# One copy and one subtraction for both heads' q or k, stacked by transfers, and attention's loads on GpSimd's queue

## The chip, the cores and the metric

The kernel runs on one core of one Trainium2 chip. The engines are TensorE (PE, with weight loads shown apart as PEld), VectorE (DVE), ScalarE (ACT), GpSimd (POOL) and SyncE (SP), which here only issues transfers. The metric is device microseconds of one execution; lower is better. A verdict is taken from several executions of both kernels on the same chip.

## The reference

A trunk of two layers on 512 positions of width 1024, batch 1, everything in float32. Each layer projects a modulated norm of x once and splits the columns among three head groups: A (4 heads, differential attention, rotary), B (6 heads, rotary, a mixture of three dilated windows) and C (6 heads, with a learned forgetting bias). Then come an output projection and a gated MLP with a causal convolution.

```
sc = jax.nn.silu(c)
for layer in range(DEPTH):
    mod = sc @ w_mod[layer] + b_mod[layer]             # 6 x 1024: shifts, scales, gates
    h = rmsnorm(x, g_attn[layer]) * (1.0 + scale1) + shift1
    proj = h @ w_in                                    # qa ka va qb kb vb qc kc vc fz
    qa, ka = apply_rope(...); qb, kb = apply_rope(...) # A and B turn q and k; C does not
    oa = diff_attention(qa, ka, va, lam)
    ob = dilated_mixture_attention(qb, kb, vb)
    oc = forgetting_attention(qc, kc, vc, cumsum(log_sigmoid(fz + forget_bias)))
    x = x + gate1 * (concat(oa, ob, oc) @ w_out)
    h = rmsnorm(x, g_mlp[layer]) * (1.0 + scale2) + shift2
    up = h @ w_up                                      # u and g, 2816 wide each
    x = x + gate2 * ((silu(conv3(g)) * u) @ w_down)
return rmsnorm(x, g_final)
```

## The kernel before

**Precision by parts.** A product of float32 values is made of three fast products: each operand is split into a high part, a copy rounded to the type that TensorE reads fast (`fp32r`), and a low part, the value less its high part. `mm3` issues high by high, low by high and high by low. A split is one copy on ACT (`split_gen`, L240; for weights L174) and one subtraction on DVE (L242; for weights L186).

**Data flow.** Activations stand as 128 features by 512 positions. Weights come from DRAM in loads of 512 KB or a little less. `Weights.dma` (L148) issues them in the fixed order of `plan` into three buffers (`raww`); `hi` and `lo` split them into `whi` and `wlo`. `pump` keeps the loads two ahead of their use. The modulation of layers 0 and 1 is computed on DVE from loads named `rawm` (L214, L217), 24 of them during layer 0's attention, the rest during the MLPs; the start of the program does the first 16 with loads named `mu`, partly with products on POOL (L1036).

**Attention.** `ORDER` pairs the sixteen heads: B0 B1 A0 C0 A1 C1 B2 C2, two heads to a pair (for A two, with two maps each). While a pair's blocks of scores, softmax and products with V run, TensorE is filled up with the projections of the next pair's q and k (`qkps`, three buffers in PSUM shared with V's projections `vps`) and of V. `qk_post` takes a projection out of PSUM and makes from it the tiles `qk` that the scores multiply. For A and B it first turns them: a copy `qf` (L456), a pair of transfers that swaps rows into `sw` (L458, L459), and three DVE operations (L462, L464, L466). Transfers are started by SP's queue, in the order of the program.

**The stacked tiles.** A score needs three products. For B and C the kernel puts two of them into one matmul by stacking 64 rows of one part over 64 rows of another. For head h of a pair, with rows R[h] of the projection:
- q of B: `res[h]` has the high part in rows R[h] and the low part in the other 64 rows.
- k of B: `res[h]` has the high part twice, `res[2+h]` the low part twice.
- C is alike, but `res[2+h]` has only one half of 64 rows, and four rows of the forgetting bias below it that come by a transfer (L443).

`stack_gen` makes these tiles with operations on 64 rows: the high part on ACT (L423), the low part on DVE (L420), and the second copies on ACT (L434, L436). B is read from `qf` in SBUF, C straight from the projection in PSUM.

**What sets the order.** Nothing is ordered by hand. The code is written as generators that are advanced in turn; a scheduler then places each engine's instructions by priority and by its own estimate of when each can start, and adds the semaphores that they need. Each transfer ends on one of eight semaphores of its kind (named DMAHW for SP's and ACT's queues, DMASW for GpSimd's), taken in turn.

In the change, `dma` (L148) and `mod_stream` (L214) name the queue of the loads, `stack_gen` is rewritten, and `layer_attn` sets the queue around its loop over blocks.

Of the kernel before, what the change touches and what calls it, by code (L numbers as in the profile page):

```python
# [8 lines left out]
F32 = mybir.dt.float32  # L9
F32R = mybir.dt.float32r  # L10
AF = mybir.ActivationFunctionType
ALU = mybir.AluOpType
# [11 lines left out]
ORDER = [(k, "AABBBCCC".index(k) + int(n)) for k, n in "B0 B1 A0 C0 A1 C1 B2 C2".split()]  # L24
# [6 lines left out]
def kernel(  # L31
# [25 lines left out]
    nc = tc.nc  # L57
    PS = bass.MemoryType.PSUM
    V, A, T, G = nc.vector, nc.scalar, nc.tensor, nc.gpsimd
# [15 lines left out]
    def tmp(name, tag):  # L75
        if tag == "rp":
            return rpp[0].tile([128, SEQ], F32, tag=tag, name=name, bufs=4)
        return tp.tile([128, SEQ], F32, tag=tag, name=name, bufs=4)
# [37 lines left out]
    for l in range(DEPTH):  # L116
# [16 lines left out]
        for m in range(KC):  # L133
            for b in range(0, FC, 8):
                n = min(8, FC - b)
                plan += [(wdown[l, m, :, 128 * b:128 * (b + n)], 128 * n, "wp" if m < 7 else "hs")]

    class Weights:
        def __init__(self):
            self.raw, self.w = {}, {}  # L140
            self.nd = self.nh = self.nl = self.nu = 0
            self.pt = None

        def dma(self, upto):
            while self.nd < min(upto, len(plan)):
                src, n, at = plan[self.nd]
                t = rawp.tile([128, 4 * VZ], F32, tag="raw", name="raww")
                nc.sync.dma_start(out=t[:, 0:n], in_=src)  # L148
                self.raw[self.nd] = t
                self.nd += 1  # L150

# [57 lines left out]
    W = Weights()  # L209

    def mod_stream(l, ci):
        part, m = divmod(ci, 8)
        raw = mrp.tile([128, 1024], F32, tag="raw", name="rawm")
        nc.sync.dma_start(out=raw, in_=wmod[l, ci])  # L214
        yield
        dst = modc[:, l, ci:ci + 1]
        V.tensor_tensor_reduce(out=raw, in0=raw, in1=scb, scale=1.0, scalar=bm[:, l, ci:ci + 1],  # L217
                               op0=ALU.mult, op1=ALU.add, accum_out=dst)
        yield
        yield  # L220
        yield
        if m < 7:
            return
        c = slice(8 * part, 8 * part + 8)
        if part in (1, 4):
            g = gA if part == 1 else gM
            V.scalar_tensor_tensor(out=scl[:, l, part // 4, :], in0=modc[:, l, c], scalar=1.0,
                                   in1=g[:, l, :], op0=ALU.add, op1=ALU.mult)
# [10 lines left out]
    def split_gen(src, hi, lo):  # L239
        A.activation(out=hi, in_=src, func=AF.Copy)  # L240
        yield
        V.tensor_tensor(out=lo, in0=src, in1=hi.bitcast(F32), op=ALU.subtract)  # L242
        yield
# [23 lines left out]
    H0, H1 = slice(0, 64), slice(64, 128)  # L267
# [98 lines left out]
    def layer_attn(l, ap, mods, st, rt0):  # L366
        h = st.h
# [45 lines left out]
                vvs[q] = ap.tile([128, 4, 4, 128], F32R, tag="vv", name="vv", bufs=2)  # L413
                aux.append(v_post(q, lambda tb: pss[tb // nb][:, 256 * (tb % nb):256 * (tb % nb) + 256]))

        def stack_gen(src, side, res, pair=None):
            R = (H0, H1)

            def sub(out, h):
                V.tensor_tensor(out=out, in0=src[R[h]], in1=res[h][R[h]].bitcast(F32), op=ALU.subtract)  # L420

            for h in range(2):
                A.activation(out=res[h][R[h]], in_=src[R[h]], func=AF.Copy)  # L423
                yield
                if side == 0:
                    sub(res[h][R[1 - h]], h)
                elif pair is None:
                    sub(res[2 + h][R[h]], h)
                else:
                    sub(res[2 + h][H0], h)  # L430
                yield
                dup = res[h][R[1 - h]] if side == 1 else res[2 + h][H0] if pair is not None else None
                if dup is not None:
                    A.activation(out=dup, in_=src[R[h]], func=AF.Copy)  # L434
                if side == 1 and pair is None:
                    A.activation(out=res[2 + h][R[1 - h]], in_=res[2 + h][R[h]].bitcast(F32), func=AF.Copy)  # L436
                yield
            if pair is not None:
                while not aug:
                    yield  # L440
                for h in range(2):
                    c = 24 * side + 4 * (2 * (pair - 5) + h)
                    nc.sync.dma_start(out=res[2 + h][64:68, :].bitcast(F32), in_=aug[0][c:c + 4, :].bitcast(F32))  # L443
                yield

        def qk_post(idx, side, ps, kind):
            n = 2 + 2 * side if kind == "B" else 4
            res = [ap.tile([128, SEQ], F32R, tag="qk", name="qk", bufs=QKB) for _ in range(n)]
            qks[idx, side] = res
            if kind == "C":  # L450
                yield from stack_gen(ps, side, res, ORDER[idx][1])
                qkdone.add((idx, side))
                return
            tb = rope_tile(kind)
            qf = tmp("qf", "rp")
            A.activation(out=qf, in_=ps, func=AF.Copy)  # L456
            sw = tmp("sw", "rp")
            nc.sync.dma_start(out=sw[0::2, :], in_=qf[1::2, :])  # L458
            nc.sync.dma_start(out=sw[1::2, :], in_=qf[0::2, :])  # L459
            for _ in range(5):  # L460
                yield
            V.tensor_tensor(out=qf, in0=qf, in1=tb[:, 0, :], op=ALU.mult)  # L462
            yield
            V.tensor_tensor(out=sw, in0=sw, in1=tb[:, 1, :], op=ALU.mult)  # L464
            yield
            V.tensor_tensor(out=qf, in0=qf, in1=sw, op=ALU.add)  # L466
            yield
            if kind != "A":
                yield from stack_gen(qf, side, res)
            else:  # L470
                hi, lo = sw.bitcast(F32R), qf.bitcast(F32R)
                yield from split_gen(qf, hi, lo)
                yield
                for m in range(4):
                    r = slice(32 * m, 32 * m + 32)
                    for j, t in enumerate((hi, lo, hi) if side == 0 else (hi, hi, lo)):
                        nc.sync.dma_start(out=res[m][32 * j:32 * j + 32, :].bitcast(F32), in_=t[r, :].bitcast(F32))
                    yield
            qkdone.add((idx, side))
# [3 lines left out]
        def rope_tile(kind):  # L483
            if kind not in rt:
                rt.clear()
                rt[kind] = load_rope(kind)
            return rt[kind]
# [102 lines left out]
        def fill(idx, share):  # L590
            f = fills[idx]
            f[2] += share * f[1]
            n = 0
            while f[0] and f[2] > 0.3:
                if next(f[0][0], StopIteration) is StopIteration:
                    f[0].pop(0)
                    continue
                f[2] -= 1.3 if getattr(f[0][0], "__name__", "") == "v_half" else 0.65
                n += 1
                tick()  # L600
            if n == 0:
                tick()
# [200 lines left out]
        emit_S(0)  # L803
        lag = 2
        f1, f2, f3 = 0.06, 0.055, 0.055
        for b in range(nb + lag):
            idx = blocks[min(b, nb - 1)][0]
            while idx and fills[idx - 1][0]:
                fill(idx - 1, 1.0)
            p = b - lag  # L810
            if l == 0 and b == 6:
                lpt.append(mrp.tile([128, 1024], F32, tag="raw", name="lp")[:, 0:256].rearrange(
                    "p (l j d) -> p l j d", l=DEPTH, j=4))
                nc.sync.dma_start(out=lpt[0], in_=lamp)
            if l == 0 and b == 10:
                with tc.issue_after(anchor[0]), tc.issue_after(anchor[1]):
                    prep()
            if b == 3:
                aux.append(after(fz_post()))
            if p >= 0:  # L820
                emit_T(p)
            if b < nb:
                emit_max(b)
            if p >= 0:
                emit_hi(p)
            fill(idx, f1)
            if b < nb:
                emit_exp(b)
            if p >= 0:
                emit_lo(p)  # L830
            fill(idx, f2)
            if b + 1 < nb:
                ready(b + 1)
                emit_S(b + 1)
            if b < nb:
                emit_norm(b)
            fill(idx, f3)
            if p >= 0:
                emit_PV(p)
            ms, mr = 4, 1.75  # L840
            if b >= ms:
                for _ in range(int((b - ms + 1) * mr) - int((b - ms) * mr)):
                    next(modg, None)
        aux.append(modg)
        for idx in range(8):
            while fills[idx][0]:
                fill(idx, 1.0)
        while any(g.__name__ == "head_post" for g in aux):
            tick()
        wl = W.use()  # L850
# [330 lines left out]
```

## Time and profile before

| what | value |
|---|---|
| median of three runs | 1337.87 us (1335.4, 1337.87, 1338.98) |
| the profiled execution | 1334.63 us, of which its span 1332.9 us |
| mean granted clock of TensorE | 0.989 |
| PE busy | 1277.8 us (96%) |
| DVE busy | 858.2 us (64%) |
| ACT busy | 642.3 us (48%) |
| POOL busy | 22.9 us (2%) |
| moved by DMA | 174.39 MB |

The profile is of one execution. Busy time of PE counts matmuls from their start to a modelled end, and they overlap, so a busy share near 100% does not say that TensorE works at its fastest pace; how many matmuls a stretch holds says more. Names such as `qkps<-hh,whi` are out<-in by the program's own tiles. In rows of groups, "x24 | 14.8, 626 | 11.5" means 24 instructions, 14.8 us busy, 626 ns each, and 11.5 us during which the engine had stood idle before them. In the timeline, a row has its start, its length, the engine and line, and in brackets the idle time ahead of it with what ended it. "SPq" is an instruction of SP that starts a transfer. The stages in the profiled execution: start to about 52 us, attention of layer 0 from there to 303, MLP to about 660, attention of layer 1 to 946, MLP to 1325, and the last norm.

### The profile page before, as it was taken

Reading aid. Unit: us, or ns where it says so; the run is one execution under the profiler, and the core shown is the slowest. Engines: PE = TensorE matmul, PEld = TensorE weight load, DVE = VectorE, ACT = ScalarE, POOL = GpSimd, SP = SyncE. Lnnn points to the kernel's source line nnn. Section 1 sums busy time; section 2 is a strip of 40 time slices with the busy share of each in tenths; the row PEclk is TensorE's granted clock in tenths of the full one; section 3 lists DMA queues with packets and bytes.
Section 4 is the critical chain, followed back from the end, with each engine's and each line's share of the span. In section 5 each row is a group of like instructions: output and inputs, shape, how many; then the busy total and the mean of one; then the engine's idle time right before and its main releaser. Section 6 shows DMA issues by size and latency. Waiting matters only on the chain.

```text
span 1332.9 us, 17722 instructions
## 1 busy us (share of the span) xinstructions
PE 1277.8 (96%) x6568; PEld 1058.6 (79%) x6568; DVE 858.2 (64%) x1600; ACT 642.3 (48%) x1158; POOL 22.9 (2%) x16
## 2 busy tenths in 40 slices
PE   4899999999999999999999999999999999999997
PEld 1788888788877778888898888878878888888886
DVE  6888999868888874423347788875754444443232
ACT  5576677745333243322336677785543333333231
POOL 5100000000000000000000000000000000000000
PEclk8899999999999999999999999999999999999999
DMA  9345454433888853332432334212133333332331
GB/s 373 140 141 183 152 180 136 130 110 129 269 261 266 267 173 95 91 103 87 117 110 95 90 103 141 66 56 90 48 109 96 97 95 95 95 91 87 103 99 63
DMA packets 56601, 174.39 MB, mean 131 GB/s; under 512 B 8130, under 2 KB 10450, under 8 KB 56516
## 3 DMA queue, kind: packets, MB, share of 16 engines
q1 hardware_dynamic: 55364, 172.16, 41.0%
q8 instruction: 52, 0.85, 0.3%
q10 hardware_dynamic: 1088, 1.05, 0.2%
q14 instruction: 33, 0.27, 0.1%
q0 software_dynamic: 64, 0.06, 0.0%
HBM read 159.41 MB, written 2.10 MB: 121 GB/s over the span
## 4 chain that ended last, share of the span: by engine, by line
PE 53%; DMA 8%; DVE 7%; ACT 4%; issue 3%; SPq 0%; DVEq 0%; ACTq 0%
DMA rawm<-in_wmod_dram 7%; PE dps L251 6%; PE dps L253 6%; PE dps L252 6%; PE pu L251 4%; PE pu L253 4%; PE pu L252 4%; PE pg L252 4%; PE pg L253 4%; PE pg L251 4%; DVE wlo L186 1%; DVE rawm L217 1%; PE qkps L251 1%; PE qkps L252 1%; PE qkps L253 1%
## 5 line engine op out<-in xcount | busy, mean ns | idle before, releaser
L186 DVE TENSOR_TENSOR wlo<-raww,whi 128x1024 fp32r<-128x1024 f32 (+3 forms) x188 | 224.2, 1193 | 241.0 <-ACT whi L174 236.5
L174 ACT ACTIVATE whi<-raww 128x1024 fp32r<-128x1024 f32 (+3 forms) x188 | 194.5, 1035 | 329.6 <-PE dps L252 137.7
L253 PE MATMUL pu<-hh,wlo 128*128 128x512 f32 (+1 forms) x368 | 141.2, 384 | 3.5 <-DVE wlo L186 3.5
L252 PE MATMUL pg<-hl,whi 128*128 128x512 f32 (+1 forms) x368 | 143.0, 389 | 1.5 <-DVE hl L300 1.5
L251 PE MATMUL pg<-hh,whi 128*128 128x512 f32 (+1 forms) x368 | 141.6, 385 | 1.6 <-ACT whi L174 1.6
L251 PE MATMUL pu<-hh,whi 128*128 128x512 f32 (+1 forms) x368 | 142.4, 387 | 0.5 <-ACT whi L174 0.5
L253 PE MATMUL pg<-hh,wlo 128*128 128x512 f32 (+1 forms) x368 | 140.9, 383 | 1.1 <-DVE wlo L186 1.1
L252 PE MATMUL pu<-hl,whi 128*128 128x512 f32 (+1 forms) x368 | 140.7, 382 | 0.0
L251 PE MATMUL dps<-mh,whi 128*128 128x512 f32 x308 | 121.5, 395 | 0.0
L253 PE MATMUL dps<-mh,wlo 128*128 128x512 f32 x308 | 121.5, 394 | 0.0
L252 PE MATMUL dps<-ml,whi 128*128 128x512 f32 x308 | 121.2, 393 | 0.0
L217 DVE CUSTOM_DVE_ANT_0 rawm<-rawm,scb,bm 128x1024 f32<-128x1024 f32 x80 | 102.3, 1279 | 23.7 <-DMA rawm<-in_wmod_dram 23.4
L654 ACT ACTIVATE e<-e,nm 128x256 f32<-128x256 f32 (+3 forms) x160 | 89.0, 557 | 33.0 <-DVE nm L641 29.9
L251 PE MATMUL qkps<-hh,whi 128*128 128x512 f32 x224 | 95.1, 424 | 4.7 <-ACT qk L434 4.1
L898 ACT ACTIVATE y<-y 128x512 f32<-128x512 f32 x44 | 27.8, 632 | 142.6 <-DVE y L895 142.6
L252 PE MATMUL qkps<-hl,whi 128*128 128x512 f32 x224 | 89.7, 400 | 0.0
L253 PE MATMUL qkps<-hh,wlo 128*128 128x512 f32 x224 | 89.6, 400 | 0.0
L253 PEld LDWEIGHTS pu<-hh,wlo 128*128 128x128 f32 x368 | 69.1, 188 | 22.1 <-DVE wlo L186 6.9
L641 DVE CUSTOM_DVE_ANT_0 e<-s,cst 128x256 f32<-128x256 f32 (+3 forms) x160 | 76.4, 481 | 12.0 <-PE s L628 3.7
L252 PEld LDWEIGHTS pg<-hl,whi 128*128 128x128 f32 x368 | 69.0, 188 | 17.7 <-DVE hl L300 3.1
L253 PEld LDWEIGHTS pg<-hh,wlo 128*128 128x128 f32 x368 | 69.0, 188 | 16.7 <-DVE wlo L186 1.9
L251 PEld LDWEIGHTS pg<-hh,whi 128*128 128x128 f32 x368 | 69.1, 188 | 16.0 <-ACT whi L174 2.0
(176 smaller groups left out, 2663.2 us busy)
## 6 DMA issues: line engine op xcount, KB each, us to landing
raww<-in_wup_dram SPq DMA_DIRECT2D x88, 512.0 KB
rawm<-in_wmod_dram SPq DMA_DIRECT2D x80, 512.0 KB
raww<-in_wqk_dram SPq DMA_DIRECT2D x32, 512.0 KB
raww<-in_wdown_dram SPq DMA_DIRECT2D x32, 512.0 KB
mu<-in_wmod_dram SPq DMA_DIRECT2D x16, 512.0 KB
raww<-in_wout_dram SPq DMA_DIRECT2D x16, 448.0 KB
raww<-in_wv_dram SPq DMA_DIRECT2D x12, 512.0 KB
raww<-in_wdown_dram SPq DMA_DIRECT2D x16, 384.0 KB
```

The lines of the kernel that those rows point to most:

```text
L174: A.activation(out=h[:, 0:m], in_=self.raw[i][:, c:c + m], func=AF.Copy)
L186: V.tensor_tensor(out=lo[:, 0:m], in0=raw[:, c:c + m], in1=h[:, 0:m].bitcast(F32), op=ALU.subtract)
L217: V.tensor_tensor_reduce(out=raw, in0=raw, in1=scb, scale=1.0, scalar=bm[:, l, ci:ci + 1], op0=ALU.mult, op1=ALU.add, accum_out=dst)
L251: T.matmul(ps[:, c], w[0], rhs[0][:, c], start=first, stop=False, skip_group_check=True)
L252: T.matmul(ps[:, c], w[0], rhs[1][:, c], start=False, stop=False, skip_group_check=True)
L253: T.matmul(ps[:, c], w[1], rhs[0][:, c], start=False, stop=last, skip_group_check=True)
L641: anchor[0] = V.tensor_tensor_reduce(out=e[:, 0:n], in0=s[:, 0:n], in1=cst[:, mask + SEQ - n:mask + SEQ], scale=-scale, scalar=3e38, op0=A ...
L654: anchor[1] = A.activation(out=e[:, 0:n], in_=e[:, 0:n], func=AF.Exp, bias=nm, scale=-1.0, accum_out=den).ins
L898: last_silu[0] = A.activation(out=y, in_=y, func=AF.Silu).ins
```

## The change

`stack_gen` no longer works on 64 rows. It makes the high and the low part of all 128 rows, both heads at once, with `split_gen` (one ACT copy, one DVE subtraction) into two plain tiles, and then fills the `qk` tiles by transfers of 64 rows by 512 (128 KB) issued from SP: four for q of B, eight for k of B, six for q or k of C. For B the two plain tiles are `sw` and `qf`, which are free by then; for C two new tiles `ch` and `cl` come from the same ring of four buffers that `qf` and `sw` use. Per layer there are three B pairs and three C pairs. ACT's operations for the stacks go from 48 to 12 a layer, DVE's from 24 to 12, and 72 transfers are added.

The queue of the weight and modulation loads becomes a variable: SP as before, but GpSimd between the start of the loop over blocks and its end, in both layers.

```diff
 class Weights:
     def __init__(self):
...
+            self.q = nc.sync
...
-                nc.sync.dma_start(out=t[:, 0:n], in_=src)
+                self.q.dma_start(out=t[:, 0:n], in_=src)
...
 def mod_stream(l, ci):
-        nc.sync.dma_start(out=raw, in_=wmod[l, ci])
+        W.q.dma_start(out=raw, in_=wmod[l, ci])
...
-        def stack_gen(src, side, res, pair=None):
+        def stack_gen(src, hi, lo, side, res, pair=None):
             R = (H0, H1)
-
-            def sub(out, h):
-                V.tensor_tensor(out=out, in0=src[R[h]], in1=res[h][R[h]].bitcast(F32), op=ALU.subtract)
-
+            yield from split_gen(src, hi, lo)
             for h in range(2):
-                A.activation(out=res[h][R[h]], in_=src[R[h]], func=AF.Copy)
-                yield
                 if side == 0:
-                    sub(res[h][R[1 - h]], h)
-                elif pair is None:
-                    sub(res[2 + h][R[h]], h)
+                    cp = [(h, R[h], hi), (h, R[1 - h], lo)] + ([(2 + h, H0, hi)] if pair is not None else [])
                 else:
-                    sub(res[2 + h][H0], h)
-                yield
-                dup = res[h][R[1 - h]] if side == 1 else res[2 + h][H0] if pair is not None else None
-                if dup is not None:
-                    A.activation(out=dup, in_=src[R[h]], func=AF.Copy)
-                if side == 1 and pair is None:
-                    A.activation(out=res[2 + h][R[1 - h]], in_=res[2 + h][R[h]].bitcast(F32), func=AF.Copy)
+                    cp = [(h, H0, hi), (h, H1, hi), (2 + h, H0, lo)] + ([(2 + h, H1, lo)] if pair is None else [])
+                for j, rows, t in cp:
+                    nc.sync.dma_start(out=res[j][rows, :].bitcast(F32), in_=t[R[h], :].bitcast(F32))
                 yield
...
             if kind == "C":
-                yield from stack_gen(ps, side, res, ORDER[idx][1])
+                hi, lo = (tmp(nm, "rp").bitcast(F32R) for nm in ("ch", "cl"))
+                yield from stack_gen(ps, hi, lo, side, res, ORDER[idx][1])
...
             if kind != "A":
-                yield from stack_gen(qf, side, res)
+                yield from stack_gen(qf, sw.bitcast(F32R), qf.bitcast(F32R), side, res)
...
+        W.q = G                    # ahead of the loop over blocks
         for b in range(nb + lag):
...
         for idx in range(8):
             while fills[idx][0]:
                 fill(idx, 1.0)
+        W.q = nc.sync
```

Three places show what the scheduler made of it. The lines of the changed file are smaller by 7 to 9 there (L251 to L253 became L252 to L254, L404 became L405, L618 became L609).

The first is POOL's own queue at the start of the program, where `bm` and `gA` are small tables and `mu` are the loads of the start. Before:

```order
L989 DMA bm<-in_bmod_dram 128x96
L989 DMA gA<-in_gattn_dram 128x16
L1036 ISA
L1036 TENSOR_TENSOR mu<-mu,scb 128x1024 [waits DMAHW5_49,Activation_49]
L1036 TENSOR_TENSOR mu<-mu,scb 128x1024 [waits DMAHW5_49]
```

and now:

```order
L982 DMA bm<-in_bmod_dram 128x96
L982 DMA gA<-in_gattn_dram 128x16
L215 DMA rawm<-in_wmod_dram 128x1024
L1029 ISA
L1029 TENSOR_TENSOR mu<-mu,scb 128x1024 [waits DMAHW5_49,Activation_49]
L1029 TENSOR_TENSOR mu<-mu,scb 128x1024 [waits DMAHW5_49]
```

The first `rawm` load, which stood behind three weight loads on SP after the start, is now issued at once, with nothing to wait for.

The second is TensorE in layer 0 where the projection of A1's q begins, during A0's last blocks (`s` scores, `pt` transposes, `po` products with V). Before:

```order
L728 MATMUL po<-pth,vv 128x256 [waits Activation_49]
L628 MATMUL s<-qk 128x384 [waits DVE_49] x2
L682 MATMUL pt<-cst,e 128x128 [waits DVE_49,PE_49]
L251 MATMUL qkps<-hh,whi 128x512 [waits Activation_49]
L729 MATMUL po<-ptl,vv 128x256 [waits DVE_49]
L728 MATMUL po<-pth,vv 128x256
```

and now:

```order
L719 MATMUL po<-pth,vv 128x256 [waits Activation_49]
L252 MATMUL qkps<-hh,whi 128x512
L253 MATMUL qkps<-hl,whi 128x512
L619 MATMUL s<-qk 128x384 [waits DVE_49]
L673 MATMUL pt<-cst,e 128x128 [waits DVE_49,PE_49]
L254 MATMUL qkps<-hh,wlo 128x512
L619 MATMUL s<-qk 128x384 [waits DVE_49]
```

The projection's first matmul waited for ACT, which means for the last copy out of C0's k in PSUM (L434); now it stands earlier and waits for nothing that is not already waited for.

The third is the beginning of layer 0's first pair, B0, on TensorE, after V's first projection. Before, three matmuls of the next projection stand ahead of the first score:

```order
L251 MATMUL qkps<-hh,whi 128x512 [waits Activation_49]
L252 MATMUL qkps<-hl,whi 128x512
L253 MATMUL qkps<-hh,wlo 128x512 [waits DVE_49]
L618 MATMUL s<-qk 128x128 [waits DMAHW3_49,DMAHW2_49,DMAHW4_49,DMAHW1_49,DMAHW5_49,DMAHW0_49,DMAHW6_49,PE_49,DMAHW7_49,Activation_49,Pool_49]
L251 MATMUL qkps<-hh,whi 128x512
L252 MATMUL qkps<-hl,whi 128x512
```

Now fifteen stand ahead of it, and this is the end of them:

```order
L252 MATMUL qkps<-hh,whi 128x512
L253 MATMUL qkps<-hl,whi 128x512
L254 MATMUL qkps<-hh,wlo 128x512
L609 MATMUL s<-qk 128x128 [waits DMAHW3_49,DMAHW4_49,DMAHW2_49,DMAHW5_49,DMAHW1_49,DMAHW6_49,DMAHW0_49,DMAHW7_49,PE_49,Pool_49]
L609 MATMUL s<-qk 128x256
L252 MATMUL qkps<-hh,whi 128x512
```

The first score moved back behind four more groups of three matmuls, and it waits for transfers where it waited for ACT. On SP at the same place, the loads of this stretch are gone after the first two, and the stacks' transfers stand there. Before:

```order
L148 DMA raww<-in_wqk_dram 128x1024 [waits DMAHW6_49]
L148 DMA raww<-in_wqk_dram 128x1024 [waits DMAHW7_49,DVE_49]
L148 DMA raww<-in_wv_dram 128x1024 [waits DMAHW0_49,DVE_49]
L214 DMA rawm<-in_wmod_dram 128x1024 [waits DMAHW1_49]
L148 DMA raww<-in_wqk_dram 128x1024 [waits DMAHW6_49,DMAHW2_49,DVE_49]
```

and now:

```order
L149 DMA raww<-in_wqk_dram 128x1024 [waits DMAHW6_49]
L149 DMA raww<-in_wqk_dram 128x1024 [waits DMAHW7_49,DVE_49]
L426 DMA qk<-sw 64x512 [waits DMAHW2_49,DMAHW3_49,DMAHW0_49,Activation_49]
L426 DMA qk<-qf 64x512 [waits DMAHW1_49,DVE_49]
L806 DMA lp<-in_lamp_dram 128x256
L426 DMA qk<-sw 64x512 [waits DMAHW5_49,DMAHW4_49,Activation_49]
L426 DMA qk<-sw 64x512
L426 DMA qk<-qf 64x512 [waits DVE_49]
```

A transfer of a high part (`sw`) waits for ACT, one of a low part (`qf`) for DVE, and each also for the transfer that last used its semaphore.

## The prediction

> **What bounds the kernel now.** I read the engines by windows first, then TensorE's waits, then single places in the timeline and the groups of the stack operations. In windows the columns are length, busy time of PE, PEld, DVE, ACT and POOL, the granted clock, the DMA share and GB/s. Here: a stretch of pure projections, then 200 us of attention in layer 0 (L0) and the same 200 us in layer 1 (L1).
>
> ```profile
> 500.00:520.00 20.00, 20.00 (x88) 16.28 (x87) 8.24 (x11) 7.04 (x9) 0.00 (x0) 1.00 0.37 106
> 62.00:262.00 200.00, 192.59 (x1167) 163.74 (x1165) 184.09 (x457) 147.35 (x333) 0.00 (x0) 0.99 0.51 160
> 706.00:906.00 200.00, 195.62 (x1200) 166.03 (x1199) 160.17 (x405) 148.03 (x333) 0.00 (x0) 1.00 0.30 92
> ```
>
> TensorE is the bound. It does 88 wide matmuls in 20 us, 227 ns each, and attention adds nothing to that work; only what makes TensorE wait there costs time. ACT is at 74% in both layers, DVE at 92% in L0 and 80% in L1. L0 did 33 matmuls fewer in 200 us, at 227 ns some 7.5 us, though both layers compute the same. That is about what there is to win in L0 beyond what L1 also loses. The waits that end on ACT or DVE, the larger ones, first L0 and then L1 (total, times, longest), with the two longest single ones in the timeline:
>
> ```profile
> PE po L728 <- ACT pth L701: 0.6, 2, 0.4
> PE s L620 <- ACT qk L436: 0.6, 2, 0.4
> PE po L729 <- DVE ptl L706: 0.4, 1, 0.4
> PE pf L537 <- DVE z L529: 0.4, 1, 0.4
> ...
> PE s L618 <- DVE nm L641: 0.9, 1, 0.9
> PE pt L682 <- ACT e L654: 0.8, 3, 0.4
> PE s L628 <- DVE nm L641: 0.6, 3, 0.2
> ...
> 130.83 0.48 PE L253 MATMUL qkps<-hh,wlo 128*128 128x512 f32 x1
> 141.51 0.57 ACT L434 ACTIVATE qk<-qkps 64x512 fp32r<-64x512 f32 x1
> 142.14 0.66 PE L251 MATMUL qkps<-hh,whi 128*128 128x512 f32 x1 [2.11 <-ACT qk L434]
> 198.50 0.50 PE L251 MATMUL qkps<-hh,whi 128*128 128x512 f32 x1 [2.04 <-ACT qk L434]
> ...
> 142.00:146.00 4.00, 3.86 (x13) 3.31 (x14) 3.53 (x11) 1.28 (x4) 0.00 (x0) 0.57 0.71 213
> 198.50:202.00 3.50, 3.50 (x19) 2.88 (x20) 3.50 (x12) 1.97 (x5) 0.00 (x0) 1.00 0.67 205
> ```
>
> C0's k lay in PSUM from the end of its projection (last matmul 130.83) until the last of its small operations (141.51 + 0.57), 11 us later; TensorE stood for that buffer, and the same again at 198.50 with C1's k. The first stall was followed by 4 us at a clock of 0.57; the second, as long, was not.
>
> **The change part by part.** Prices of the stack operations, removed ones first, then the two shapes that replace them:
>
> ```profile
> L423 ACT ACTIVATE qk<-qf 64x512 fp32r<-64x512 f32 x24 | 14.8, 626 | 11.5 <-DVE qf L466 11.1
> L434 ACT ACTIVATE qk<-qkps 64x512 fp32r<-64x512 f32 x24 | 14.2, 592 | 3.4 <-DVE qk L420 2.8
> L423 ACT ACTIVATE qk<-qkps 64x512 fp32r<-64x512 f32 x24 | 14.1, 587 | 0.3
> L434 ACT ACTIVATE qk<-qf 64x512 fp32r<-64x512 f32 x12 | 7.5, 629 | 0.2
> L436 ACT ACTIVATE qk<-qk 64x512 fp32r<-64x512 f32 x12 | 7.5, 624 | 0.2
> L420 DVE TENSOR_TENSOR qk<-qkps,qk 64x512 fp32r<-64x512 f32 x24 | 16.5, 687 | 1.6 <-ACT qk L423 1.1
> L420 DVE TENSOR_TENSOR qk<-qf,qk 64x512 fp32r<-64x512 f32 x24 | 16.4, 685 | 1.0 <-ACT qk L423 0.5
> L456 ACT ACTIVATE qf<-qkps 128x512 f32<-128x512 f32 x20 | 11.4, 582 | 1.5 <-PE qkps L253 1.3 <-ACT whi L174 0.2
> L466 DVE TENSOR_TENSOR qf<-qf,sw 128x512 f32<-128x512 f32 x20 | 13.6, 682 | 0.1
> ```
>
> 128 rows cost what 64 rows cost. ACT loses 96 operations (58.1 us) and gains 24: twelve from PSUM at 0.582 and twelve from SBUF at 0.626, 14.5 us; net -43.6 us, half in each layer. DVE goes from 48 (32.9 us) to 24 (16.4 us), -16.5 us. None of this is on TensorE, so it counts only through waits.
>
> (a) The PSUM stalls. A C projection is now out of PSUM after one copy and one subtraction instead of seven or more small operations, and in the new order the matmul behind C0's k waits for nothing. I take off both stalls, 4.1 us, and the slow clock, 0.43 x 4 = 1.7: -5.8. Ends: -4.1 (the dip comes elsewhere) to -5.8. In the Trainium skill, "TensorE: Matmul & The Clock Gate", section "Part 1: The HAM clock gate", the clock falls only after an idle window of about 3.4 us; by that rule a wait of 2.1 us would not have caused the dip, the dip would stay, and the sum would come to -4.5 instead of -6.2. The row at 142 shows the dip right behind the wait, the row at 198.50 a like wait without it, so the trace does not settle it.
>
> (b) The other waits on ACT and DVE. Without the L436 wait, which goes into (c), the rows above hold 1.4 us in L0 and 2.3 in L1, 3.7 together. ACT has 15% less to do there (21.8 of 147), DVE 5%. Since half of the waits name DVE, and each hangs on one softmax step and not on a full queue, I take half: -1.9. Ends 0 and -3.7.
>
> (c) The transfers. There are 72 a layer from SP. What one costs, and what it stands in for, in the next rows: a swap's landing, and the issue and landing of C's bias rows (both end on a DMA and are followed in the chain of waits, start and length); then B0's two waiting operations and first scores; last, the same place for C2 in L1.
>
> ```profile
> 801.07 3.41 DMA sw<-qf
> 813.49 0.59 SPq L477
> 814.12 1.78 DMA qk<-sw
> ...
> 64.62 0.22 PE L618 MATMUL s<-qk 128*128 128x128 f32 x1
> 65.80 0.63 ACT L436 ACTIVATE qk<-qk 64x512 fp32r<-64x512 f32 x1
> 66.48 0.33 PE L620 MATMUL s<-qk 128*128 128x128 f32 x1
> ...
> 894.18 0.59 ACT L434 ACTIVATE qk<-qkps 64x512 fp32r<-64x512 f32 x1
> 894.82 0.33 PE L618 MATMUL s<-qk 128*128 128x128 f32 x1 [0.27 <-ACT qk L434]
> ```
>
> In eight of twelve B and C pairs (B0, B1, B2, C2 of each layer) the first score starts within half a microsecond of the last stack operation, as in the first and last shown. There the new chain counts. For k of a B pair's first head it is four issues at 0.59 and a landing of 1.78 to 3.41, 4.1 to 5.8 us, where three operations of 0.6 stood (1.9): 2.3 to 3.9 us longer. But the new order puts other matmuls ahead of these scores. At B0 of L0 it is twelve, 2.7 us at 227 ns; counted the same way for all eight, 1.9 to 4.7 us, mean 3.1. That is the middle of the lengthening, so I take 0. Low end: -0.6, the L436 wait, which vanishes with its operation. High end: landing 3.41 and one other issue ahead on SP, 4.5 us longer in all, less each place's own delay: 0.6 to 2.6 us, +12 over eight places. New waits elsewhere: SP holds the next swap's transfers behind a stack's while it waits for its high and low parts (one operation of 0.6 and one of 0.7, with PE fed by filler meanwhile); ACT's `ch` copy waits for the transfers that still read its ring buffer, two stacks earlier, some 24 matmuls or 5 us. Both I cost at nothing; without that cover they are part of the +12. The transfers' bytes, 18.9 MB in all, add to a DMA share of 0.51 and 0.30.
>
> (d) The first `rawm` load starts at once, among the start's own loads, where memory is the bound:
>
> ```profile
> 20.00:40.00 20.00, 8.85 (x20) 4.83 (x18) 20.00 (x26) 6.42 (x11) 18.32 (x8) 0.66 0.91 353
> ```
>
> 512 KB at 353 GB/s is +1.5 us. Ends 0 (it goes beside them) and +1.5.
>
> (e) 73 loads are issued by POOL. The thinnest cover of any of them, and the price of POOL's issue:
>
> ```profile
> 92.50 0.33 SPq L214 DMA_DIRECT2D rawm<-in_wmod_dram  x1
> 96.48 1.27 DVE L217 CUSTOM_DVE_ANT_0 rawm<-rawm,scb,bm 128x1024 f32<-128x1024 f32 x1
> ...
> 1.25 0.70 POOL L989 DMA_DIRECT2D bm<-in_bmod_dram  x1 [0.80 <-POOLq L1170]
> ```
>
> This load was read 4.0 us after its issue without DVE standing idle for it; the weights are read later still. An issue on POOL is 0.37 us longer, POOL has nothing else to do there, and SP is freed for the stacks: 0. If DVE waits, PE has the filler between.
>
> The sum against the profiled execution: -5.8 - 1.9 + 0 + 1.5 + 0 = -6.2, 1334.6 to 1328.4. That execution lies 3.2 us under the median of the three runs, so against the median: 1337.9 - 6.2 = 1331.7, or 0.46% less. A difference of 0.3% (4.0 us) is about what a measurement can tell from none.
>
> **Rivals.** R1: the gains do not reach the end. The 7.5 us between the layers may belong to L0's DVE at 92%, not to PSUM, and the matmul that starts earlier meets the next wait on DVE. Left are (d) and a few tenths: 1336 to 1339, no change. Against it: the stall's releaser is exact to 0.06 us.
>
> R2, slower: the transfers are late at the eight places, 1.5 us each on the mean, +12: 1343.7. It decides from a mean lateness of 1.3 us on, which brings the sum past 1341.9. For it: the landing rows span 1.8 to 3.4, and L0's DMA share was 0.71 just at 142. Against it: the new order's delay.
>
> R3: POOL's work on a load holds DVE. POOL on the same buffers stretched one of DVE's operations, as the start shows:
>
> ```profile
> 19.48 18.65 POOL L1036 TENSOR_TENSOR mu<-mu,scb 128x1024 f32<-128x1024 f32 x7 [7.83 <-DMA mu<-in_wmod_dram]
> 25.97 2.52 DVE L300 SCALAR_TENSOR_TENSOR hl<-ht,modc,hh 128x512 fp32r<-128x512 f32 x1
> 40.86 0.75 DVE L300 SCALAR_TENSOR_TENSOR hl<-ht,modc,hh 128x512 fp32r<-128x512 f32 x1
> ```
>
> 48 loads in L0 at 0.70 are 33.6 us of POOL; at the stretch of 2.52 for 0.75 DVE would lose 23.6 us of them, against 16 us idle in the window's 200 and 7 won (half of 16.5, over 200 of 240 us). (b) is gone (+1.9), and I estimate a quarter of the 23.6 on the path (+5.9): 1339.5. In the Trainium skill, "SBUF — State Buffer", section "Who interferes with whom", a DVE operation with two SBUF inputs contends with a GpSimd instruction that reads SBUF, not with one that only writes; by that, issuing loads would cost DVE nothing. The L300 rows agree with its first half; no run here shows the second. The same section says that a DVE operation can starve GpSimd of the time to make descriptors, which no run here shows either.
>
> **How the numbers follow.** The forecast has 0.55, with its own range 1327.8 (all low ends, -10.1) to 1334. R1 has 0.23, R2 0.15, R3 0.07. Slower are nearly all of R2 and a little of R3, 0.16; no change R1, most of R3 and the forecast's upper edge, 0.28; faster the rest, 0.56. The range goes from 1325 (1327.8, less the 2.5 us by which the fastest run lay under the median) to 1341.5, which leaves out most of R2.
>
> **What would show it.** (a) No `qkps` matmul waits on an ACT copy out of `qkps`, and the clock at the former 142 is near 1.00. (b) ACT about 44 us and DVE 16 us less busy over the span; L0 holds nearer 1200 matmuls in its 200 us. (c) 144 more issues on SP; scores that wait name `DMA qk`, below 0.5 us each; over 1.3 us each means R2. (d) The first projection starts 1.5 us later. (e) POOL shows 73 more issues; no wait of PE ends on a load; stretched DVE rows in attention mean R3. The forecast is wrong if the same microseconds return as waits on softmax steps (R1), or if scores stand for transfers.

## The result, and the profile after

The changed kernel is slower: 1353.33 us in the median of four runs (1349.44 to 1357.25), where the kernel before had 1337.98. The ratio is 1.0118, with a 95% interval of 1.0078 to 1.0158. The profiled execution took 1350.23 us, its span is 1348.2.

Busy times of the page, then the two attention windows of 200 us (columns as before: length, PE, PEld, DVE, ACT, POOL, clock, DMA share, GB/s):

```profile
PE 1284.4 (95%) x6568; PEld 1066.9 (79%) x6568; DVE 841.6 (62%) x1576; ACT 599.0 (44%) x1086; POOL 62.4 (5%) x90
...
62.00:262.00 200.00, 188.93 (x1122) 162.41 (x1122) 168.79 (x426) 121.06 (x282) 24.18 (x46) 0.96 0.72 195
706.00:906.00 200.00, 192.98 (x1210) 168.66 (x1209) 148.10 (x385) 121.57 (x284) 11.44 (x22) 0.98 0.51 135
```

ACT lost 43 us of work over the span and DVE 16.6, as worked out. Yet layer 0 (L0) did 45 matmuls fewer than before in the same 200 us, and the clock of its window went from 0.99 to 0.96. TensorE's waits in attention, L0 and then layer 1 (L1), in total, times, longest, and with them DVE's wait for the swaps of L0, before and after:

```profile
PE po L719 <- ACT e L645: 5.7, 2, 3.5
PE s L611 <- DMA qk<-qf: 2.2, 1, 2.2
PE s L613 <- DMA qk<-aT: 1.7, 1, 1.7
...
PE s L611 <- DMA qk<-qf: 3.1, 2, 2.6
PE s L609 <- DVE z L515: 1.7, 1, 1.7
PE s L613 <- DMA qk<-aT: 1.4, 2, 1.1
...
DVE qf L462 <- DMA sw<-qf: 0.5, 2, 0.3
DVE qf L453 <- DMA sw<-qf: 10.1, 6, 3.4
```

The stalls for PSUM are gone. In their place scores stand for transfers (`qk<-aT` are C's bias rows, the others the stacks). The largest row, two waits that are named after a softmax step, comes from DVE: it does its work in order, and the softmax step's reductions stood behind a rotation whose swap had not landed. Before, DVE waited 0.5 us in all for L0's swaps, now 10.1. The longest such place, DVE and then TensorE:

```profile
233.02 0.69 DVE L453 TENSOR_TENSOR qf<-qf,rope 128x512 f32<-128x512 f32 x1 [3.40 <-DMA sw<-qf]
238.06 0.55 PE L719 MATMUL po<-pth,vv 128*128 128x256 f32 x1 [3.55 <-ACT e L645]
...
234.00:238.00 4.00, 0.51 (x3) 0.07 (x1) 4.00 (x11) 2.36 (x5) 0.00 (x0) 0.81 0.21 49
238.00:242.00 4.00, 3.94 (x12) 3.43 (x13) 3.79 (x7) 1.29 (x4) 0.53 (x1) 0.50 0.89 193
```

TensorE stood 3.55 us, and the 4 us behind it ran at a clock of 0.50, which is another 2 us of its full pace. Not every wait is followed by such a stretch: behind the other wait of that row, 2.11 us at 128.33, the clock stayed at 1.00. What a transfer of a kind took from its issue to its landing (the last number, a median):

```profile
qk<-ch SPq DMA_DIRECT2D x48, 128.0 KB, 5.5
sw<-qf SPq DMA_DIRECT2D x40, 128.0 KB, 3.4
qk<-qf SPq DMA_DIRECT2D x36, 128.0 KB, 5.4
qk<-cl SPq DMA_DIRECT2D x24, 128.0 KB, 4.8
```

The stages, in us from the profiled executions. They are cut at the first V projection of each layer, the last output projection and the last down projection, so they are the same work in each row. Here stand also the experiments that the next section tells:

| kernel | start | L0 attention | L0 MLP | L1 attention | span | ratio to before (95%) |
|---|---|---|---|---|---|---|
| before | 52.2 | 254.8 | 380.9 | 263.0 | 1332.9 | |
| after | 53.4 | 265.7 | 380.3 | 266.9 | 1348.2 | 1.0118 (1.0078 to 1.0158) |
| e1: old stacks, loads on GpSimd | 53.9 | 270.7 | 382.3 | 265.6 | 1355.0 | 1.0152 (1.0137 to 1.0168) |
| e2: new stacks, loads on SP | 52.7 | 251.9 | 378.5 | 258.7 | 1323.7 | 0.9903 (0.9888 to 0.9918) |
| e6: new stacks, all on GpSimd | 53.7 | 254.5 | 379.8 | 265.1 | 1336.2 | 1.0003 (0.9984 to 1.0022) |
| e10: old stacks, all on GpSimd | 53.6 | 255.8 | 380.4 | 263.1 | 1334.9 | 1.0006 (0.9995 to 1.0018) |
| e11: as e6, from each layer's beginning | 54.2 | 250.9 | 379.7 | 261.7 | 1328.8 | 0.9972 (0.9961 to 0.9982) |

### The profile page after: what moved, and what is told of

It is laid out like the page before. It is cut to its first block, busy times and chain, and to the rows that moved or that the text cites. A ratio compares the mean times of both kernels' runs of the same rounds, so it can differ in the third digit from the quotient of the medians.

```text
span 1348.2 us, 17969 instructions
## 1 busy us (share of the span) xinstructions
PE 1284.4 (95%) x6568; PEld 1066.9 (79%) x6568; DVE 841.6 (62%) x1576; ACT 599.0 (44%) x1086; POOL 62.4 (5%) x90
## 4 chain that ended last, share of the span: by engine, by line
PE 57%; DMA 9%; DVE 4%; issue 3%; ACT 1%; SPq 1%; DVEq 0%; ACTq 0%
DMA rawm<-in_wmod_dram 7%; PE dps L252 6%; PE dps L254 6%; PE dps L253 6%; PE pu L252 4%; PE pu L254 4%; PE pu L253 4%; PE pg L253 4%; PE pg L254 4%; PE pg L252 4%; PE qkps L252 2%; PE qkps L253 2%; PE qkps L254 2%; DMA qk<-qf 1%; DVE rawm L218 1%
## 5 line engine op out<-in xcount | busy, mean ns | idle before, releaser
L253 PE MATMUL pg<-hl,whi 128*128 128x512 f32 (+1 forms) x368 | 143.0, 389 | 1.5 <-DVE hl L301 1.5
L254 PE MATMUL pu<-hh,wlo 128*128 128x512 f32 (+1 forms) x368 | 141.3, 384 | 3.2 <-DVE wlo L187 3.2
L252 PE MATMUL pg<-hh,whi 128*128 128x512 f32 (+1 forms) x368 | 141.5, 385 | 1.6 <-ACT whi L175 1.6
L252 PE MATMUL pu<-hh,whi 128*128 128x512 f32 (+1 forms) x368 | 142.4, 387 | 0.1
L254 PE MATMUL pg<-hh,wlo 128*128 128x512 f32 (+1 forms) x368 | 140.9, 383 | 1.1 <-DVE wlo L187 1.1
L253 PE MATMUL pu<-hl,whi 128*128 128x512 f32 (+1 forms) x368 | 140.7, 382 | 0.0
L252 PE MATMUL dps<-mh,whi 128*128 128x512 f32 x308 | 121.5, 394 | 0.0
L254 PE MATMUL dps<-mh,wlo 128*128 128x512 f32 x308 | 121.5, 394 | 0.0
L253 PE MATMUL dps<-ml,whi 128*128 128x512 f32 x308 | 121.2, 393 | 0.0
L252 PE MATMUL qkps<-hh,whi 128*128 128x512 f32 x224 | 97.2, 434 | 0.8
L253 PE MATMUL qkps<-hl,whi 128*128 128x512 f32 x224 | 91.0, 406 | 0.0
L254 PE MATMUL qkps<-hh,wlo 128*128 128x512 f32 x224 | 90.9, 406 | 0.0
L254 PEld LDWEIGHTS pu<-hh,wlo 128*128 128x128 f32 x368 | 69.1, 188 | 22.3 <-DVE wlo L187 7.1
L253 PEld LDWEIGHTS pg<-hl,whi 128*128 128x128 f32 x368 | 69.0, 188 | 17.7 <-DVE hl L301 3.1
L254 PEld LDWEIGHTS pg<-hh,wlo 128*128 128x128 f32 x368 | 69.0, 188 | 16.6 <-DVE wlo L187 1.9
L252 PEld LDWEIGHTS pg<-hh,whi 128*128 128x128 f32 x368 | 69.1, 188 | 16.0 <-ACT whi L175 2.0
```

The costliest lines, as they stand in the source:

```text
L252: T.matmul(ps[:, c], w[0], rhs[0][:, c], start=first, stop=False, skip_group_check=True)
L253: T.matmul(ps[:, c], w[0], rhs[1][:, c], start=False, stop=False, skip_group_check=True)
L254: T.matmul(ps[:, c], w[1], rhs[0][:, c], start=False, stop=last, skip_group_check=True)
```

## The experiments

### The two halves of the change apart

Theory L: the loads on a queue of their own keep the other transfers from landing. Theory T: the 144 new transfers do it themselves. Theory B: it takes both.

The loads alone, in the kernel before:

```diff
-                nc.sync.dma_start(out=t[:, 0:n], in_=src)
+                self.q.dma_start(out=t[:, 0:n], in_=src)     # likewise in mod_stream
+        W.q = G          # ahead of the loop over blocks, nc.sync again behind it
```

> The stacks as before; only the weight and modulation loads of attention are issued from GpSimd's queue. Theory L (the loads on a queue of their own start beside the swaps and keep DVE and the scores waiting): most of the loss of the changed kernel is here, 1346 to 1352 us. Theory T (the 144 transfers land late and fill the DMA engines, whoever issues the loads): 1338 to 1340, with at most the 1.2 us that the start is later. Theory B (it takes both, loads that overtake and transfers that are in the way): 1338 to 1342.

Measured: 1356.1 us, ratio 1.0152 (1.0137 to 1.0168), 4 us above what theory L had.

The stacks alone:

```diff
-        W.q = G
```

> The stacks by transfers as in the changed kernel, with all loads on SP as before. Theory L: the loss goes, 1331 to 1337 us, as the prediction had it. Theory T: 1347 to 1353, as the changed kernel. Theory B: 1339 to 1344, with DVE's waits on the swap (10.1 us in layer 0 after the change) mostly gone and scores still waiting on transfers.

Measured: 1323.45 us, ratio 0.9903 (0.9888 to 0.9918). This is the fastest kernel of the study, 8 us below what theory L had. In its direction theory L holds, though both its ranges were missed: the stacks by transfers gain 1.0%, the loads on GpSimd's queue cost 1.5% with the old stacks and 2.2% (1.0118 / 0.9903) with the new. The same kinds of transfer, with all loads on SP:

```profile
qk<-ch SPq DMA_DIRECT2D x48, 128.0 KB, 2.5
sw<-qf SPq DMA_DIRECT2D x40, 128.0 KB, 2.0
qk<-qf SPq DMA_DIRECT2D x36, 128.0 KB, 2.9
qk<-cl SPq DMA_DIRECT2D x24, 128.0 KB, 4.9
```

The first three land in about half of the time; C's low parts (`qk<-cl`) take as long as before. DVE waits for no swap in L0's loop, and the scores' waits on transfers are these two:

```profile
PE s L609 <- DMA qk<-sw: 1.4, 1, 1.4
...
PE s L609 <- DMA qk<-qf: 0.3, 1, 0.3
```

The DMA engines were hardly busier in the slow kernel: the share of L0's window is 0.72 after and 0.69 here, with fewer bytes moved (195 against 207 GB/s). So it is not the amount of bytes.

What the loss is made of shows in L0's attention as a whole, first after the change, then here:

```profile
53.39:319.05 265.66, 252.76 (x1502) 218.36 (x1501) 208.33 (x497) 150.80 (x338) 25.84 (x49) 0.96 0.64 176
52.72:304.64 251.92, 245.31 (x1502) 212.02 (x1501) 209.51 (x497) 150.38 (x338) 0.00 (x0) 0.99 0.62 187
```

Both hold the same 1502 matmuls. Of the 13.7 us between them, TensorE's idle time is 6.3 (12.9 against 6.6). Its clock is about 8, an estimate from the rounded clock: 0.04 of 266 us against 0.01 of 252. So the slow stretches cost no less than the waits themselves.

### Is it GpSimd, or is it a second queue?

Theory Q: a load on another queue than a swap takes the DMA engines beside it, while on the swap's own queue a load that is issued later stays behind it. Theory G: what GpSimd starts is slow, or takes the engines in itself. Four kernels tell them apart. First everything of attention on GpSimd's queue, with the new stacks (e6) and with the old ones (e10):

```diff
-            nc.sync.dma_start(out=sw[0::2, :], in_=qf[1::2, :])
+            W.q.dma_start(out=sw[0::2, :], in_=qf[1::2, :])     # and all transfers into qk
```

> The changed kernel with the swaps and stack transfers of attention on GpSimd's queue too, behind and ahead of the loads as they are issued. Theory Q (two queues: a load issued beside or after a swap takes the DMA engines from it, which on one queue it cannot): most of the loss goes, 1324 to 1334 us, DVE's waits on the swap in layer 0 under 4 us. Theory G (what GpSimd's queue starts is slow or takes the engines in itself): 1345 to 1365.

> The stacks as in the kernel before, with attention's loads and also its swaps and A's transfers on GpSimd's queue: the run with only the loads on GpSimd's queue, made one queue again. Theory Q: most of its 19 us goes, 1335 to 1345 us, the swap's landing near 2 us and DVE's waits on it under 6 us. Theory G: it stays at 1353 to 1360.

Measured: e6 1336.96 us, ratio 1.0003 (0.9984 to 1.0022); e10 1337.89 us, 1.0006 (0.9995 to 1.0018). With the old stacks all of the 1.5% is gone, though 48 loads and more are still issued by POOL in L0. That speaks for Q and leaves nothing to G there. With the new stacks most of the loss goes, but e6 stays 3 us above theory Q's range.

Next the queues exchanged, loads on SP and transfers on GpSimd (e7), and the loads on ACT's queue (e9, `W.q = A`):

> The other way round: all loads on SP, the swaps and stack transfers on GpSimd's queue. Theory Q: two queues again, 1340 to 1356 us, with DVE waiting for swaps. Theory G: the 512 KB loads are off GpSimd's queue, 1323 to 1333.

> The changed kernel with the loads of attention on ACT's queue in place of GpSimd's. Theory Q: a second queue whatever the engine, 1340 to 1355 us, landings of the swap near 3.5 us. Theory G: 1323 to 1333, landings near 2. ACT also spends some 0.3 us on an issue and holds its work while a load waits for its buffer, up to +5 us by either.

Measured: e7 1364.14 us, ratio 1.0205 (1.0184 to 1.0226), slower still than the range of either theory, and no run tells why it is slower than the changed kernel; e9 1349.83 us, 1.0086 (1.0053 to 1.0118). Two queues are slow whichever engine has the loads. The swap's landing in these runs, in the order e1, e9, e7 (two queues), e6, e10 (one queue; the few swaps ahead of the loop are left out):

```profile
sw<-qf SPq DMA_DIRECT2D x40, 128.0 KB, 3.9
```
```profile
sw<-qf SPq DMA_DIRECT2D x40, 128.0 KB, 4.2
```
```profile
sw<-qf POOLq DMA_DIRECT2D x40, 128.0 KB, 3.3
```
```profile
sw<-qf POOLq DMA_DIRECT2D x32, 128.0 KB, 2.1
```
```profile
sw<-qf POOLq DMA_DIRECT2D x32, 128.0 KB, 2.6
```

3.3 to 4.2 us with two queues, 2.0 to 2.6 with one. DVE's waits for L0's swaps go with it: 12.6 us in e1, 9.8 in e9 and 7.7 in e7, but 0.8 in e6 and 0.7 in e10. The stacks' transfers are not slowed in every case: in e9 `qk<-ch` lands in 2.4 us and `qk<-qf` in 2.6, about as in e2. One place shows it close by, the seventh swap of L0 (its second half is the row `sw<-qf`, the reader is DVE's row). First the kernel before, then e1, then e10:

```profile
155.64 0.58 SPq L459 DMA_DIRECT2D sw<-qf  x1
156.32 0.54 SPq L214 DMA_DIRECT2D rawm<-in_wmod_dram  x1
...
158.50 0.69 DVE L462 TENSOR_TENSOR qf<-qf,rope 128x512 f32<-128x512 f32 x1
```
```profile
163.58 0.58 SPq L460 DMA_DIRECT2D sw<-qf  x1
...
163.47 0.53 POOL L215 DMA_DIRECT2D rawm<-in_wmod_dram  x1 [1.37 <-DVE modc L218]
...
169.13 0.69 DVE L463 TENSOR_TENSOR qf<-qf,rope 128x512 f32<-128x512 f32 x1 [2.83 <-DMA sw<-qf]
```
```profile
158.32 0.54 POOL L460 DMA_DIRECT2D sw<-qf  x1
158.86 0.54 POOL L215 DMA_DIRECT2D rawm<-in_wmod_dram  x1
...
161.01 0.69 DVE L463 TENSOR_TENSOR qf<-qf,rope 128x512 f32<-128x512 f32 x1
```

On one queue, SP's or GpSimd's, the `rawm` load of 512 KB follows the swap by 0.5 to 0.7 us, and DVE reads the swap 2.7 to 2.9 us after its second half was issued, without waiting. On two queues the load starts 0.1 us ahead of that half, and the swap is there only after 5.5 us, of which DVE stood 2.83. The order of the work is not the cause at this place: the thirteen operations of DVE ahead of it, from a weight split (`wlo`, at 159.81 in e1 and 154.56 in e10) on, are the same in the same order, and each starts 5.25 to 5.26 us later in e1 than in e10. The Trainium skill has the rule, "DMA: Bandwidth & Descriptors", section "Queues, rings and completion order": every DMA engine goes in turn between the queues that have work for it, a packet at a time, and takes the work of one queue in its order. The landings above agree with it (3.3 to 4.2 us against 2.0 to 2.6); that the turns are by packets no run here shows.

### How much each kind of load does

```diff
-        W.q.dma_start(out=raw, in_=wmod[l, ci])
+        nc.sync.dma_start(out=raw, in_=wmod[l, ci])
```

> The changed kernel with the modulation loads (rawm, 24 of the 73) back on SP, the weight loads still on GpSimd's. Layer 1 has no modulation loads in its attention and lost less. If the loss goes by the number of loads beside swaps (theory Q): 1333 to 1345 us, and the start is again as before. If the weights alone cause it, since only they feed TensorE: 1347 to 1353.

Measured: 1342.92 us, ratio 1.0033 (1.0014 to 1.0051). The 24 `rawm` loads on GpSimd's queue account for 0.8% (1.0118 less 1.0033), the 50 weight loads (24 `wqk`, 12 `wv`, 14 of the output projection in the trace, one more than counted ahead) for 1.3% (1.0033 / 0.9903). The start is back at 52.2 us: the early `rawm` load cost 1.2 us there. It goes roughly by the number of loads, and not only by those that feed TensorE.

### What is left with everything on GpSimd's queue

e6 is still 1.0% slower than e2, its twin on SP.

```diff
+        W.q = G          # at the beginning of layer_attn
...
-        W.q = G          # ahead of the loop over blocks
```

> The run with everything of attention on GpSimd's queue lost 13 us to the one with everything on SP. There the first stacks and loads of each layer (B0) were still split over the two queues, and the scores of B0 stood 2.7 us in layer 0 and 1.6 and 2.6 us in layer 1. Here the switch to GpSimd's queue is made at the beginning of each layer's attention, so that B0's are on one queue too; the first weight loads of layer 0 then stand behind POOL's products at the start, which can cost a few us there. Theory Q: layer 1's attention from 265.1 to 258 to 261 us (258.7 with all on SP). If GpSimd's queue itself is what costs, it stays at 264 to 267.

Measured: 1332.11 us, ratio 0.9972 (0.9961 to 0.9982), L1's attention 261.7 us: 3.4 less than e6, just outside what theory Q had it at, and 3.0 above e2. A part of e6's rest was B0's split over two queues: in L1, scores waited 3.5 us for transfers in e6 and 0.3 in e11. The medians of e11 and e2 are still 8.7 us apart. Between the two profiled executions it is 5.1, in the start (1.5), the first MLP (1.2) and L1 (3.0), while L0 is 1.0 shorter in e11; no run tells what the rest is, and GpSimd's own cost may be among it.

### The stacks: which part gains

C's q and k first copied out of PSUM whole, in the kernel before:

```diff
+                cf = tmp("cf", "rp")
+                A.activation(out=cf, in_=ps, func=AF.Copy)
+                yield
-                yield from stack_gen(ps, side, res, ORDER[idx][1])
+                yield from stack_gen(cf, side, res, ORDER[idx][1])
```

> The kernel before, with one more ACT copy of C's q and k out of PSUM (12 copies of 0.6 us over both layers), from which the 64-row operations then read. It tests step (a) alone: if the two stalls of 2.1 us and the slow clock behind the first are what the PSUM buffer costs, 1331 to 1334 us and no wait of a qkps matmul on ACT's stack operations. If another wait takes their place, 1336 to 1340.

Measured: 1335.22 us, ratio 0.9993 (0.9981 to 1.0006): no difference, and between the two ranges. L0's largest waits there are:

```profile
PE s L621 <- DVE nm L644: 2.4, 3, 1.7
PE qkps L253 <- DVE wlo L186: 1.4, 2, 0.7
```

The PSUM stalls are gone, and TensorE waits for DVE in their place, 3.8 us for the 4.1 that went.

Now only C's stacks by transfers (e4), and only B's (e5), both with all loads on SP and the old `stack_gen` for the other:

> C's stacks by transfers (24 a layer... 72 over both layers), B's as before, all loads on SP. Theory T: about half of the loss of the run with all stacks by transfers, or less, since C's scores come later than B's: 1338 to 1345. Theory L: 1331 to 1335, since the PSUM stall is gone and B's first scores wait for nothing new. Theory B: 1334 to 1340.

> B's stacks by transfers, C's as before, all loads on SP. The PSUM stalls of C's k stay possible. If C's share (1328.4 with C alone by transfers) and B's add up to the 1323.5 of both, B alone is 1330 to 1334; if B's scores wait for their transfers and only C's part gains, 1336 to 1341; if the gain is only the work taken from ACT and DVE, half each, 1328 to 1332.

Measured: e4 1328.37 us, ratio 0.9939 (0.9924 to 0.9953); e5 1329.74 us, 0.9956 (0.9939 to 0.9972). e4 is below all of its ranges. The two gains, 0.6% and 0.4%, add up to e2's 1.0%, and e5 is also where it was expected (1328 to 1332) if the gain is only the work taken from ACT and DVE; the two runs don't tell these apart. e5 gains although it keeps the two PSUM stalls, as its row and L0's window show:

```profile
PE qkps L252 <- ACT qk L454: 3.1, 2, 2.0
...
62.00:308.00 246.00, 238.28 (x1449) 204.04 (x1447) 212.09 (x505) 159.80 (x355) 0.00 (x0) 1.00 0.55 168
```

## Why the prediction was wrong

The step that failed is (e), the loads on POOL at nothing. It was costed by the readers of the loads, and for them it was right: no wait of TensorE in attention ends on a load, so the sign that was named for (e) held while the step failed. What was left out is what the one queue did for the others. With the loads on SP the swaps landed in 2.0 us (e2); with the loads on a queue of their own they took 3.4 (after), and moving the loads cost 2.2% (after against e2), some 30 us. The text named SP's relief as a gain of the move; the order on SP was worth more.

The others, by their letters:

- (a) -5.8 was too much. The stalls went as described, but e3, which takes them away with little else, measures -0.07% (-0.2 to +0.1%): the wait moved to DVE, as R1 had it. The slow clock should not have been in it: e5 has stalls of 2.0 and 1.1 us and a clock of 1.00 over L0, and e2, without the stalls, has 4 us at 0.57 in another place (190 to 194). The rule that the prediction weighed, from the Trainium skill, "TensorE: Matmul & The Clock Gate", section "Part 1: The HAM clock gate", left the dip in and so came nearer in the price, but the traces do not bear it out: after the change the clock was 0.51 for the 3.4 us behind a wait of 2.23 us (at 72.57) and 1.00 behind one of 2.11 (at 128.33).
- (b) -1.9 was too small. e5 gains 0.44%, 5.9 us, with the stalls in place, so for B alone the relief of ACT and DVE and the new order together are worth about that; no run separates the two. The waits with names were a poor measure of it: they held 3.7 us in all.
- (c) 0 was near: with the loads on SP, scores wait 1.7 us for transfers in the whole program. That the filler which the new order puts ahead covered the lengthening by 2.3 to 3.9 us fits this, but no run takes the filler away. Steps (a) to (c) together were forecast at -7.7, and e2 measured -13 (0.97% of 1337).
- (d) +1.5 held: the first projection starts 1.14 us later (26.67 instead of 25.53).
- R2 gave a time of 1343.7 for late transfers, and the transfers were late. But the cause was another, the loads, and the place only in part the one it named: scores stood 5.3 us for the stacks' transfers (B0 in both layers, B1 in layer 1) where R2 had 12, and 7.4 us, with the longest single wait, came through DVE. R3 did not happen: DVE's rows keep their lengths, for example the sum over `rawm` (1279 ns before, in the 80 of the program):

```profile
L218 DVE CUSTOM_DVE_ANT_0 rawm<-rawm,scb,bm 128x1024 f32<-128x1024 f32 x80 | 102.3, 1280 | 23.2 <-DMA rawm<-in_wmod_dram 22.5
```

What stays open: a queue change also changes the scheduler's order of the work (in the traces, e1's order on DVE shares 96% of its sequence with that of before, e10's 90%). The landings show the loss physically, and e10, whose order is the more changed, is back at the time before; but how much of the 1.5 to 2.2% each of the two makes up was not separated over the whole program.

## What to carry to other kernels

In this kernel, moving large loads to a queue of their own took away the protection that one queue in order gave to small transfers on the path. Before such a move, list what else is in flight on the DMA engines at that time, who waits for it, and how much slack it has, and look not only at when the load itself is read. Small transfers that replace work on busy engines can pay, if they stay on the queue on which the large loads stand behind them.

## What the runs showed of the hardware

A second queue slowed the swaps whether GpSimd or ACT issued the loads (3.9 and 4.2 us in e1 and e9, against 2.0 with all on SP), and a single queue on GpSimd served them about as fast as SP's (2.1 in e6). An issue of a load on POOL took 0.53 us, against 0.33 for one on SP. And idle time of TensorE can cost more than its length: behind the wait of 3.55 us the granted clock was 0.50 for 4 us. The length of the wait alone does not tell whether that happens: behind 2.23 us it did, behind 2.11 us it did not.
